# Sums of the down projection parked in DRAM between its pieces, and one more group of seven products, in a hybrid DiT step on one Trainium2 core

## The chip, the cores and the metric

One NeuronCore of a Trainium2 chip runs the whole program. The metric is the device time of one execution in microseconds (us); of the kernel before three executions were timed, and one further execution was profiled.

## What is computed

One inference step of a diffusion backbone with one layer, for two groups of 128 tokens (context and latent) of width 2048, all in fp32: modulation from a conditioning vector, one input projection, two attention mixers, their merge, and then the part that the change touches, a squared-ReLU MLP of width 8192:

```python
h2 = rms_norm(x, norm2_w) * (1 + sc2) + sh2
x = x + g2 * (jnp.square(jax.nn.relu(h2 @ w_up)) @ w_down)
```

The products keep nearly fp32 precision: every operand is split into a high part that fp32r holds exactly and a low part (the rest), and one product of two 128-row tiles is three matmuls: high by high, high by low, low by high.

## The kernel before, in words

All weights stream once from DRAM in tiles of 128 x 1024 fp32 (512 KB). One such tile is a **step**, and the kernel first writes a list of 456 steps (`wsteps`) and then records them in order in `run`. A step has a load (`raw`, in SyncE's queue, SP), a preparation (ScalarE copies `raw` to `wH`, L103; VectorE subtracts to `wL`, L269) and its matmuls. Two strings of digits set how far the recording runs ahead: at step i the loads up to step i + 4 + `RUN[i]` are issued and the preparations up to step i + `LOOK[i]` are recorded. All engines run their queues in order, and all tiles live in one pool of 50 buffers of 4 KB per partition (`G`), so a load waits in SP's queue until the buffer that it was given is free. For a few steps the low part is made by a GpSimd DMA that adds into it (`LO_DMA`), or the high part is loaded by a GpSimd DMA (`HI_DMA`, empty before).

The MLP is cut into eight pieces of 1024 hidden columns. After the up projection of piece 0, for p = 0 to 6, the up projection of piece p + 1 (`up_pair`, a **pair**, 16 steps) comes ahead of the down projection of piece p (`down_unit`, four units n = 0 to 3 of four steps each, one for each 512 output columns), and the down projection of piece 7 ends the program. So pair 1 is steps 216 to 231, down projection 0 steps 232 to 247, pair 2 steps 248 to 263, down projection 1 steps 264 to 279, pair 3 steps 280 to 295, and so on in 32s.

A pair has eight groups of two steps. A **plain** group does 8 products (24 matmuls) from two `wH`/`wL` tiles. A **fast** group forms sums of weight and activation blocks so that 7 products (21 matmuls, into Q1 to Q7) do the work of 8, in Winograd's manner; ScalarE makes `XH`, half of `YB`, `tH` and `uH`, and VectorE the other half of `YB`, `t`, `XL`, `tL`, `uL` and two half-width sums (L1315 to L1325). `FAST` names the places (0 to 7) of the fast groups in each pair: 34 fast groups in all.

The down projection's partial sums, 128 x 1024 for each n, are carried from piece to piece. ScalarE copies the two PSUM banks of a finished unit into `dsum[n]`, and three steps ahead of the next piece's unit n (`SEED_AT`; for n = 0 at the end of the pair) it copies them back into PSUM (`seed`), where the next matmuls add to them. So four of the 50 buffers hold `dsum` through the whole MLP.

Beside this, VectorE works off dot products of the conditioning vector with columns of the modulation weights (L1476, tiles `aT`), one job of two instructions per entry of `DOTS`/`DOTS2`, which give the step.

In the input projection `SEED1` says for each unit of a later chunk whether its earlier sum is copied into PSUM ahead of it by ScalarE, or added after it by VectorE.

Of the kernel before, what the change touches and what calls it, by code (L numbers as in the profile page):

```python
# [10 lines left out]
F32 = mybir.dt.float32  # L11
# [7 lines left out]
P = 128  # L19
# [12 lines left out]
LOAD = 4  # L32
FB_DVE = 2
FB1 = 10
H_AT = 3
FILL = {1: [("gB", 2), ("gB", 3)], 3: [("gB", 0), ("gB", 1)]}
DOTS1 = [9, 11, 14, 19, 22, 24, 25, 27, 28, 30, 32, 33, 34, 35, 37, 40, 41, 42, 44, 46, 48, 49, 51, 53]
CHUNKS = [2, 2, 2, 4, 6]
NFAST = 8
FAST = {1: (0, 2, 5, 7), 2: (0, 4, 5, 6, 7), 3: (0, 2, 4, 5, 7), 4: (0, 2, 4, 5, 7), 5: (0, 1, 3, 4, 7), 6: (0, 3, 4, 5, 7), 7: (0, 1, 3, 6, 7)}  # L40
SEED_AT = 3
QK_ACT = [('qB', 1)]
H2_DVE = [(0, 1), (0, 3), (1, 1), (1, 3)]
KEEP = True
ROWS_AT = [8, 11, 7]
SEED1_AT = 2
SEED1 = "111110100100111111011111111001011111"
BACK = 9
AWAY = [('gA', 1), ('gB', 2), ('gB', 3), ('gA', 0), ('gB', 0), ('gA', 2)]
GATE_BACK = 1  # L50
# [1 line left out]
LO_DMA = [50, 54, 56, 63, 77, 107, 129, 144, 145, 176, 184, 188, 189, 203, 228, 233, 250, 286, 297, 360, 388, 392, 403, 447]  # L52
LO_AHEAD = 2

LOOK = "610013015100121312024402233324102425654224523344556654121016645565652437574377445343414661516353205210022636320000411134313643044023400458230315565645456443574337324421522555644666784051000205311111322534111433455554321045445111013410444324654734331001335565775443654453304436533423355423455542233213213545587654334232213213202440122544412433432313432443523324313211333435533333213331314344422557756822145342656433332302254541454475574464555546763333345544"
RUN = "345110004667224234111350007998421004464200022565595544243214333434399864346555377654224635443144230021224242114401324405201346530331035587986564665545676867644543555342013141147676676965699967265287998988511453877787785653022200123446553345324545104653232464345673321110102122521121211202355533232133432223443232410110000000011234344212022112531112752123301000112323643331133410100122454235566436675432012021222210010001154457832224556577677636445664422134"
CONST_AT = [83, 79]
XL_DMA = [8]
HI_DMA = []
ADA_AT = [None, 4, 13, 22, 25]  # L60
XS_AT = {1: 3, 2: 25, 3: 34}
POST = {('kvA', 0): [81, 83, 89], ('qA', 0): [84, 86, 92], ('qA', 1): [84, 86, 90], ('kB', 0): [88, 92, 96], ('qB', 0): [94, 98, 104], ('kB', 1): [98, 101, 103], ('qB', 1): [102, 106, 107]}
# [2 lines left out]
T_AT = [4, 4]  # L65
PREP_IN = [5, 7]
DOTS = [44, 58, 58, 61, 62, 63, 65, 66, 66, 66, 69, 70, 71, 71, 72, 74, 76, 81, 84, 85, 89, 91, 94, 96, 96, 96, 100, 100, 101, 102, 102, 105, 107, 107, 107, 110, 110, 111, 113, 114, 115, 117, 117, 117, 120, 120, 120, 121, 121, 123, 123, 124, 127, 128, 128, 132, 132, 133, 133, 134, 135, 136, 141, 143, 144, 144, 149, 151, 151, 152, 157, 157, 157, 162, 163, 170, 172, 174, 174, 174, 176, 176, 178, 182, 183, 187, 190, 190]
DOTS2 = [224, 231, 231, 233, 235, 237, 238, 242, 245, 263, 265, 269, 275, 296, 299, 304, 309, 329, 331, 331, 333, 333, 353, 360, 362, 364, 366, 368, 382, 391, 394, 396]
STAT_AT = [-2, -1, 8, 17]
T_PAIR = [[7, 10], [6, 9], [8, 9], [8, 9], [10, 14], [10, 10], [11, 14]]  # L70
P_PAIR = [[5, 5], [2, 2], [2, 4], [6, 2], [4, 2], [4, 4], [6, 0]]
M_TE = (3,)
M_AT = [4, 6, 9]
FLIP = 1
P_UP = [2, 3]
T_UP = [6, 12]
COL = {"qA": 0, "kvA": 1024, "qB": 1536, "kB": 2560, "vB": 3584, "gA": 4608, "gB": 6656}


# [1 line left out]
def tile_hybrid_step(ctx: ExitStack, tc: tile.TileContext, a):  # L81
# [8 lines left out]
    dp = ctx.enter_context(tc.tile_pool(name="dram", bufs=1, space=bass.MemoryType.DRAM))  # L90
    act, dve, pe, pool, sync = nc.scalar, nc.vector, nc.tensor, nc.gpsimd, nc.sync

    def G(name, dt=F32):
        return gp.tile([P, 1024], dt, name=name, tag="g")
# [4 lines left out]
    def bank(name, pool_=None):  # L99
        return (pool_ or paux).tile([P, 512], F32, name=name, tag="b")  # L100

    def copy(out, in_):
        act.activation(out, in_, AF.Copy)  # L103
# [112 lines left out]
    wsteps = []  # L216
    cal = {}

    def at(i, fn):
        cal.setdefault(i, []).append(fn)  # L220
# [9 lines left out]
    def add_step(src, mm, key, half=0):  # L230
# [409 lines left out]
    def unit(w, c0, ktiles, stat, evac, key, seeded=None):  # L640

        box = {}
        n = len(ktiles)
        for j, k0 in enumerate(ktiles):
            def mm(st, j=j):
                if j == 0 and st["half"] == 0:
                    box["acc"] = seeded() if seeded else [bank("acc", pacc) for _ in range(2)]
                mm3(box["acc"], stat(j), st, j == 0 and st["half"] == 0 and not seeded, j == n - 1 and st["half"] == 1,
                    bool(seeded))
                if j == n - 1 and st["half"] == 1:  # L650
                    evac(box["acc"])
            add_w(w, k0, c0, mm, key)
# [323 lines left out]
    def up_flip(n):  # L976
        flip(("a", n))
# [45 lines left out]
    for u in AWAY:  # L1023
        i = end_of(("y" + u[0][1].lower(), u[1]))
# [156 lines left out]
    def up_unit(n):  # L1181
# [66 lines left out]
    def up_pair(p):  # L1248
        n0, n1 = PIECES[p]
        w, box, key = a["w_up"], {"begun": set()}, ("up", n0)  # L1250
        fast = FAST[p]

# [28 lines left out]
        for pos, is_fast in enumerate(kinds):  # L1281
# [16 lines left out]
            def prep_x(b=b, pos=pos):  # L1298
                b["XH"] = b["x"].pop("hi", None)
                if b["XH"] is None:  # L1300
                    b["XH"] = G("XH", F32R)
                    copy(b["XH"], b["x"]["raw"])
                if 8 * p + pos in XL_DMA:
                    b["XL"] = G("XL", F32R)
                    minus_plus(b["XL"], b["XH"], b["x"]["src"])

            def prep_y(b=b, pos=pos):
# [11 lines left out]
                dve.tensor_tensor(Y[:, 0:512], t[:, 0:512], X[:, 512:1024], op=OP.add)  # L1319
                if 8 * p + pos not in XL_DMA:  # L1320
                    dve.tensor_tensor(b["XL"], X, b["XH"].bitcast(F32), op=OP.subtract)
# [50 lines left out]
            for i, (nm, pf, mf) in enumerate((("x", prep_x, mm_x), ("y", prep_y, mm_y))):  # L1372
# [4 lines left out]
                else:  # L1377
                    assert wsteps[-1]["i"] not in HI_DMA
                wsteps[-1]["prep"] = pf

    dsum = {}
    last = len(PIECES) - 1

    def out_s(acc, n, ss, c=slice(0, 512)):
# [2 lines left out]
            out = a["y_prompt"] if s == 0 else a["y_sample"]  # L1387
            sync.dma_start(out[0][:, n * 512 + c.start:n * 512 + c.stop], x1[n][:, s, c])

    seeds = {}  # L1390

    def seed(p, n):

        seeds[p, n] = [bank("acc", pacc) for _ in range(2)]
        for s in range(2):
            copy(seeds[p, n][s], dsum[n][:, s, :])
        if p == last:
            dsum.pop(n)

    def down_unit(p, n):  # L1400
        def evac(acc):
            if p == 0:
                dsum[n] = G(f"dsum{n}").rearrange("p (s n) -> p s n", s=2)
            if p == last:
                out_s(acc, n, range(2))
                return
            for s in range(2):
                copy(dsum[n][:, s, :], acc[s])

        def stat(j):  # L1410
            return lambda kk, tb: (aH[PIECES[p][j]][:, kk, tb, :], aL[PIECES[p][j]][:, kk, tb, :])

        def seeded():
            if (p, n) not in seeds:
                seed(p, n)
            return seeds.pop((p, n))
        if p and (n or p == last):
            at(len(wsteps) - SEED_AT, lambda: seed(p, n))
        if p == last and n == 3:
            last_unit(a["w_down"], 512 * n, [4 * j for j in PIECES[p]], stat, lambda acc, s, *c: out_s(acc, n, [s], *c), ("down", p, n), seeded)  # L1420
            return
        unit(a["w_down"], 512 * n, [4 * j for j in PIECES[p]], stat, evac, ("down", p, n), seeded if p else None)

    for n in PIECES[0]:
        up_unit(n)
    for n in range(4):
        at(end_of(("up", 0)) + 1 + n, lambda n=n: x1_away(n))
    for g in range((max(len(f) for f in FAST.values()) + 1) // 2):
        at(end_of(("up", 0)) + STAT_AT[g], lambda g=g: fast_stat(g))
    for p in range(len(PIECES)):  # L1430
        if p < last and p + 1 not in FAST:
            for n in PIECES[p + 1]:
                up_unit(n)
        elif p < last:
# [106 lines left out]
    i = ROWS_AT[0] + max(i for i, (job, h, n) in placed if job[0] == "g1")  # L1541
# [115 lines left out]
```

## Time and profile before

| | |
|---|---|
| time, median of 3 executions | 1315.3 us (1315.15 to 1315.69) |
| profiled execution: its time / span of its instructions | 1315.33 / 1313.6 us |
| TensorE (PE) busy | 1300.4 us, 99% |
| VectorE (DVE) busy | 1147.2 us, 87% |
| ScalarE (ACT) busy | 918.3 us, 70% |
| DMA packets of the weights' queue | 378.18 MB, 78.8% of 16 engines' span |

The page's slices of 1/40 show where an engine is full, the windows the same for chosen stretches, the lines what one instruction costs, and the waits what held an engine or a queue up. A matmul's shown duration overlaps the next one's, so its price is the distance from start to start.

### The profile page before, as it was taken

Reading aid. Unit: us, or ns where it says so; the run is one execution under the profiler, and the core shown is the slowest. Engines: PE = TensorE matmul, PEld = TensorE weight load, DVE = VectorE, ACT = ScalarE, POOL = GpSimd, SP = SyncE. Lnnn points to the kernel's source line nnn. Section 1 sums busy time; section 2 is a strip of 40 time slices with the busy share of each in tenths; the row PEclk is TensorE's granted clock in tenths of the full one; section 3 lists DMA queues with packets and bytes.
Section 4 is the critical chain, followed back from the end, with each engine's and each line's share of the span. In section 5 each row is a group of like instructions: output and inputs, shape, how many; then the busy total and the mean of one; then the engine's idle time right before and its main releaser. Section 6 shows DMA issues by size and latency. Waiting matters only on the chain.

```text
span 1313.6 us, 17446 instructions
## 1 busy us (share of the span) xinstructions
PE 1300.4 (99%) x5978; PEld 1051.6 (80%) x5978; DVE 1147.2 (87%) x1531; ACT 918.3 (70%) x1299; POOL 60.9 (5%) x67
## 2 busy tenths in 40 slices
PE   8999999999999999999999999999999999999998
PEld 4677888888777788888888888888888888888886
DVE  4578999999999999999879998897989998979653
ACT  5656766698865566645687857869678687796881
POOL 0000000341100000000000000000000000000000
PEclk9999999999999999999999999999999999999999
DMA  9999998898899999999398775888586697867692
GB/s 372 408 408 409 378 363 320 314 339 287 294 338 364 411 377 353 363 353 379 104 331 305 256 252 173 280 286 285 198 302 226 209 319 249 295 160 303 195 352 79
DMA packets 148313, 393.80 MB, mean 300 GB/s; under 512 B 51680, under 2 KB 52672, under 8 KB 148224
## 3 DMA queue, kind: packets, MB, share of 16 engines
q1 hardware_dynamic: 144064, 378.18, 78.8%
q0 software_dynamic: 4016, 14.42, 5.7%
q8 instruction: 47, 0.77, 0.2%
q14 instruction: 42, 0.34, 0.1%
q10 hardware_dynamic: 144, 0.08, 0.0%
HBM read 373.97 MB, written 8.70 MB: 291 GB/s over the span
## 4 chain that ended last, share of the span: by engine, by line
PE 64%; DVE 4%; issue 1%; DVEq 0%
PE acc L321 13%; PE acc L322 13%; PE acc L320 13%; PE Q L1260 6%; PE Q L1258 6%; PE Q L1259 6%; DVE junk L1476 1%; DVE aT L1476 1%; DVE wL L269 1%; PE Z L1260 1%; PE Z L1258 1%; PE Z L1259 1%; PE acc L1096 1%; PE acc L1095 1%; PE acc L1078 1%
## 5 line engine op out<-in xcount | busy, mean ns | idle before, releaser
L269 DVE TENSOR_TENSOR wL<-raw,wH 128x1024 fp32r<-128x1024 f32 x361 | 425.6, 1223 | 63.9 <-ACT wH L103 63.0
L103 ACT ACTIVATE wH<-raw 128x1024 fp32r<-128x1024 f32 (+1 forms) x391 | 388.2, 1044 | 59.7 <-DMA raw<-in_w_br_a 8.4
L1476 DVE SCALAR_TENSOR_TENSOR aT<-aT,cB 128x1024 f32<-128x1024 f32 x144 | 173.7, 1222 | 1.1
L1476 DVE SCALAR_TENSOR_TENSOR junk<-aT,cB 128x1024 bf16<-128x1024 f32 x144 | 173.7, 1223 | 0.0
L451 PE MATMUL acc<-wH,hH 128*128 128x512 f32 x276 | 108.2, 392 | 0.0
L453 PE MATMUL acc<-wH,hL 128*128 128x512 f32 x276 | 107.5, 389 | 0.0
L452 PE MATMUL acc<-wL,hH 128*128 128x512 f32 x276 | 107.4, 389 | 0.0
L103 ACT ACTIVATE uH<-raw 128x1024 fp32r<-128x1024 f32 x34 | 36.1, 1063 | 65.1 <-DVE raw L1322 59.5
L451 PEld LDWEIGHTS acc<-wH,hH 128*128 128x128 f32 x276 | 51.8, 188 | 13.9 <-issue 2.5
L453 PEld LDWEIGHTS acc<-wH,hL 128*128 128x128 f32 x276 | 51.8, 188 | 10.8
L452 PEld LDWEIGHTS acc<-wL,hH 128*128 128x128 f32 x276 | 51.8, 188 | 10.6
L103 ACT ACTIVATE tH<-t 128x1024 fp32r<-128x1024 f32 x34 | 36.0, 1058 | 29.0 <-DVE t L1315 26.8
L320 PE MATMUL acc<-wH,hH 128*128 128x512 f32 x128 | 52.7, 411 | 0.0
L321 PE MATMUL acc<-wL,hH 128*128 128x512 f32 x128 | 50.2, 392 | 1.3 <-DVE wL L269 1.3
L486 PE MATMUL acc<-wH,hH 128*128 128x512 f32 x128 | 50.5, 395 | 0.0
L487 PE MATMUL acc<-wL,hH 128*128 128x512 f32 x128 | 50.0, 391 | 0.3 <-DVE wL L269 0.2
L322 PE MATMUL acc<-wH,hL 128*128 128x512 f32 x128 | 50.0, 391 | 0.0
L488 PE MATMUL acc<-wH,hL 128*128 128x512 f32 x128 | 49.9, 390 | 0.0
L1325 DVE TENSOR_TENSOR uL<-raw,uH 128x1024 fp32r<-128x1024 f32 x34 | 41.7, 1225 | 1.1
L1315 DVE TENSOR_TENSOR t<-raw 128x1024 f32<-128x1024 f32 x34 | 41.4, 1218 | 1.3 <-PE Q L1259 1.3
L1324 DVE TENSOR_TENSOR tL<-t,tH 128x1024 fp32r<-128x1024 f32 x34 | 41.4, 1217 | 0.0
L103 ACT ACTIVATE acc<-dsum 128x512 f32<-128x512 f32 x56 | 31.6, 590 | 13.8 <-DVE up L1360 7.1
(648 smaller groups left out, 3337.7 us busy)
## 6 DMA issues: line engine op xcount, KB each, us to landing
raw<-in_w_in SPq DMA_DIRECT2D x133, 512.0 KB, 8.2
raw<-in_w_down SPq DMA_DIRECT2D x128, 512.0 KB, 6.0
aT<-in_w_adaT SPq DMA_DIRECT2D x80, 512.0 KB, 8.4
raw<-in_w_upF SPq DMA_DIRECT2D x68, 512.0 KB, 5.3
aT<-in_w_gT SPq DMA_DIRECT2D x64, 512.0 KB, 8.0
raw<-in_w_up SPq DMA_DIRECT2D x60, 512.0 KB, 6.2
araw<-in_w_pair SPq DMA_DIRECT2D x48, 512.0 KB, 9.2
raw<-in_w_out SPq DMA_DIRECT2D x32, 512.0 KB, 9.6
```

The costliest lines, as they stand in the source:

```text
L103: act.activation(out, in_, AF.Copy)
L269: dve.tensor_tensor(st["lo"], st["raw"], st["hi"].bitcast(F32), op=OP.subtract)
L320: pe.matmul(acc[tb], sh, wh[:, k, :], start=f, stop=False, skip_group_check=seeded)
L321: pe.matmul(acc[tb], sh, wl[:, k, :], start=False, stop=False, skip_group_check=seeded)
L322: pe.matmul(acc[tb], sl, wh[:, k, :], start=False, stop=l, skip_group_check=seeded)
L451: pe.matmul(acc[tb], sh, wh[:, k, :], start=opened[u] and k == 0, stop=False, skip_group_check=skip)
L452: pe.matmul(acc[tb], sh, wl[:, k, :], start=False, stop=False, skip_group_check=skip)
L453: pe.matmul(acc[tb], sl, wh[:, k, :], start=False, stop=last and k == 1, skip_group_check=skip)
L1258: pe.matmul(acc, stat[0], hi, start=f, stop=False)
L1259: pe.matmul(acc, stat[0], lo, start=False, stop=False)
L1260: pe.matmul(acc, stat[1], hi, start=False, stop=l)
L1476: dve.scalar_tensor_tensor(out, box["raw"], 1.0, cB[s, tag], op0=OP.mult, op1=OP.mult, accum_out=dst[:, s, fb:fb + 1])
```

## The change

The sums of a unit are now copied into a new buffer `dpart`, stored to DRAM six steps after the unit (`SUM_AWAY`), and loaded again ten steps ahead of the unit that goes on with them (`SUM_BACK`), all in SP's queue. That is so for the down projections 0 to 5; what down projection 6 leaves stays in SBUF as before. Pair 2 has one more fast group, at its place 2 (steps 252 and 253), which makes 35; in pair 7 the fast group at place 6 moves to place 4. The high part of step 234 comes by a GpSimd DMA. `LOOK` changes in 51 places, 35 of them in steps 239 to 289, and `RUN` in 60: in steps 238 to 294 it changes at 52 and rises at 44 of them (for the 16 steps of down projection 1 it reads 3211101021225211 before and 1685756597166055 after), and outside that stretch only eight digits change, by one. Four dot jobs move later, from steps 245, 263, 265 and 275 to 265, 265, 267 and 279. Of the input projection's second chunk one unit (`qB`, 0) is added by VectorE instead of copied in ahead. `H_AT` enters a maximum that another term decides.

```diff
-H_AT = 3
+H_AT = 4
...
-FAST = {1: (0, 2, 5, 7), 2: (0, 4, 5, 6, 7), 3: (0, 2, 4, 5, 7), 4: (0, 2, 4, 5, 7), 5: (0, 1, 3, 4, 7), 6: (0, 3, 4, 5, 7), 7: (0, 1, 3, 6, 7)}
+FAST = {1: (0, 2, 5, 7), 2: (0, 2, 4, 5, 6, 7), 3: (0, 2, 4, 5, 7), 4: (0, 2, 4, 5, 7), 5: (0, 1, 3, 4, 7), 6: (0, 3, 4, 5, 7), 7: (0, 1, 3, 4, 7)}
...
-SEED1 = "111110100100111111011111111001011111"
+SEED1 = "111010100100111111011111111001011111"
...
+SUM_AWAY = 6
+SUM_BACK = 10
...
-HI_DMA = []
+HI_DMA = [234]
...
-T_PAIR = [[7, 10], [6, 9], [8, 9], [8, 9], [10, 14], [10, 10], [11, 14]]
+T_PAIR = [[7, 10], [6, 9], [8, 9], [8, 10], [10, 14], [10, 10], [11, 14]]
...
-T_UP = [6, 12]
+T_UP = [6, 14]
...
     def seed(p, n):
 
         seeds[p, n] = [bank("acc", pacc) for _ in range(2)]
         for s in range(2):
             copy(seeds[p, n][s], dsum[n][:, s, :])
-        if p == last:
-            dsum.pop(n)
+        dsum.pop(n)
+
+    def sum_away(p, n):
+        dmem[n] = dp.tile([P, 1024], F32, name=f"dm{p}_{n}")
+        sync.dma_start(dmem[n], parts.pop(n).rearrange("p s n -> p (s n)"))
+
+    def sum_back(n):
+        t = G(f"dsum{n}")
+        sync.dma_start(t, dmem.pop(n))
+        dsum[n] = t.rearrange("p (s n) -> p s n", s=2)
 
     def down_unit(p, n):
+        if 0 < p < last:
+            i = len(wsteps) - SUM_BACK
+            assert i > sum_end[n] + SUM_AWAY
+            at(i, lambda: sum_back(n))
         def evac(acc):
-            if p == 0:
-                dsum[n] = G(f"dsum{n}").rearrange("p (s n) -> p s n", s=2)
             if p == last:
                 out_s(acc, n, range(2))
                 return
+            t = G(f"dpart{n}").rearrange("p (s n) -> p s n", s=2)
             for s in range(2):
-                copy(dsum[n][:, s, :], acc[s])
+                copy(t[:, s, :], acc[s])
+            (dsum if p == last - 1 else parts)[n] = t
...
         unit(a["w_down"], 512 * n, [4 * j for j in PIECES[p]], stat, evac, ("down", p, n), seeded if p else None)
+        if p < last - 1:
+            sum_end[n] = len(wsteps) - 1
+            at(sum_end[n] + SUM_AWAY, lambda: sum_away(p, n))
```

The first place is SP's queue from the end of down projection 0's loads through those of pair 2 to the first ones of down projection 1 (`upF` is a fast group's weights, `up` a plain one's). Before:

```order
L243 DMA raw<-in_w_upF 128x1024 x2
L243 DMA raw<-in_w_up 128x1024 x6
L243 DMA raw<-in_w_upF 128x1024 x8
L243 DMA raw<-in_w_down 128x1024 x2
L1463 DMA aT<-in_w_gT 128x1024
```

With the change, from the first store on, which stands behind the first two `upF` and one `up` (`dm_n` is the place in DRAM of sum n):

```order
L1403 DMA dm_0_6976<-dpart_6829 128x1024
L245 DMA raw<-in_w_up 128x1024
L245 DMA raw<-in_w_upF 128x1024 x2
L245 DMA raw<-in_w_up 128x1024 x2
L245 DMA raw<-in_w_upF 128x1024
L1403 DMA dm_1_7086<-dpart_6930 128x1024
L245 DMA raw<-in_w_upF 128x1024 x4
L1403 DMA dm_2_7152<-dpart_7026 128x1024
L245 DMA raw<-in_w_upF 128x1024 x3
L245 DMA raw<-in_w_down 128x1024 x2
L1403 DMA dm_3_7272<-dpart_7112 128x1024
L1407 DMA dsum_7288<-dm_0_6976 128x1024
```

The four stores stand between pair 2's loads, and the first sum's return stands behind the second load of down projection 1. The same pattern comes for each of the six down projections, 48 DMAs in all.

The second place is VectorE's queue at the start of pair 2's preparations (`t` to `uL` is a fast group, `wL` half of a plain one, `aT` and `junk` half of a dot job). Before:

```order
L269 TENSOR_TENSOR wL<-raw,wH 128x1024
L1315 TENSOR_TENSOR t_7021<-raw 128x1024
L1318 TENSOR_TENSOR YB<-raw,YB 128x512
L1319 TENSOR_TENSOR raw<-t_7021,raw 128x512
L1321 TENSOR_TENSOR XL<-raw,XH 128x1024
L1322 TENSOR_TENSOR raw<-raw 128x512
L1324 TENSOR_TENSOR tL<-t_7021,tH 128x1024
L1325 TENSOR_TENSOR uL<-raw,uH 128x1024
L1476 SCALAR_TENSOR_TENSOR aT,gc_g_362<-aT,cB_6289 128x1024
L1476 SCALAR_TENSOR_TENSOR junk,gc_g_362<-aT,cB_6287 128x1024
L1476 SCALAR_TENSOR_TENSOR aT,gc_g_362<-aT,cB_6289 128x1024
L269 TENSOR_TENSOR wL<-raw,wH 128x1024 x5
```

With the change, from the end of the first fast group:

```order
L1327 TENSOR_TENSOR uL<-raw,uH 128x1024
L271 TENSOR_TENSOR wL<-raw,wH 128x1024
L1317 TENSOR_TENSOR t_7172<-raw 128x1024
L1320 TENSOR_TENSOR YB<-raw,YB 128x512
L1321 TENSOR_TENSOR raw<-t_7172,raw 128x512
L1323 TENSOR_TENSOR XL<-raw,XH 128x1024
L1324 TENSOR_TENSOR raw<-raw 128x512
L1326 TENSOR_TENSOR tL<-t_7172,tH 128x1024
L1327 TENSOR_TENSOR uL<-raw,uH 128x1024
L271 TENSOR_TENSOR wL<-raw,wH 128x1024 x2
```

The new fast group's seven instructions stand where two `wL` and the dot halves stood; the dot halves come later. (Step 250's low part is one of those that GpSimd makes, so a `wL` fewer than steps is seen in both.)

## Rows read from the trace of the kernel before

**Rows 1.** The page: span, the engines' busy time, granted clock in 40 slices, DMA rate.
```profile
span 1313.6 us, 17446 instructions
...
PE 1300.4 (99%) x5978; PEld 1051.6 (80%) x5978; DVE 1147.2 (87%) x1531; ACT 918.3 (70%) x1299; POOL 60.9 (5%) x67
...
PEclk9999999999999999999999999999999999999999
...
GB/s 372 408 408 409 378 363 320 314 339 287 294 338 364 411 377 353 363 353 379 104 331 305 256 252 173 280 286 285 198 302 226 209 319 249 295 160 303 195 352 79
```

**Rows 2.** Windows; stretch: its length, busy us of each engine, clock, DMA share, GB/s.
```profile
40.00:400.00 360.00, 356.60 (x1704) 284.19 (x1701) 327.39 (x501) 260.71 (x535) 40.83 (x34) 1.00 0.94 350
...
660.00:1220.00 560.00, 560.00 (x2472) 463.35 (x2471) 504.55 (x574) 428.68 (x477) 8.72 (x10) 1.00 0.78 260
```

**Rows 3.** Windows of down projection 0, pair 2, down projection 1 and pair 3.
```profile
719.00:763.00 44.00, 44.00 (x196) 36.44 (x195) 42.21 (x56) 35.97 (x37) 0.86 (x1) 1.00 0.80 263
763.00:804.00 41.00, 41.00 (x183) 33.95 (x182) 39.30 (x44) 24.24 (x29) 0.00 (x0) 1.00 0.64 236
804.00:848.00 44.00, 44.00 (x195) 36.21 (x194) 36.77 (x44) 39.96 (x46) 0.00 (x0) 1.00 0.69 232
848.00:889.00 41.00, 41.00 (x183) 33.95 (x182) 38.62 (x43) 26.72 (x30) 1.73 (x2) 1.00 0.86 290
```

**Rows 4.** Timeline of PE inside pair 3: start, us, engine, line, instruction.
```profile
852.85 0.39 PE L1258 MATMUL Q<-wH,h22H 128*128 128x512 f32 x1
...
853.30 0.39 PE L1260 MATMUL Q<-wH,h22L 128*128 128x512 f32 x1
```

**Rows 5.** Lines of DVE, 719 to 848 us: busy us, mean ns of one, idle before.
```profile
L269 DVE TENSOR_TENSOR wL<-raw,wH 128x1024 fp32r<-128x1024 f32 x34 | 39.8, 1219 | 4.6 <-ACT wH L103 4.6
L1476 DVE SCALAR_TENSOR_TENSOR aT<-aT,cB 128x1024 f32<-128x1024 f32 x12 | 14.6, 1222 | 0.2
...
L1325 DVE TENSOR_TENSOR uL<-raw,uH 128x1024 fp32r<-128x1024 f32 x6 | 7.4, 1225 | 0.3
...
L1318 DVE TENSOR_TENSOR YB<-raw,YB 128x512 fp32r<-128x512 f32 x6 | 4.1, 685 | 1.0 <-ACT YB L103 1.0
```

**Rows 6.** Lines of ACT, 719 to 848 us.
```profile
L103 ACT ACTIVATE wH<-raw 128x1024 fp32r<-128x1024 f32 x37 | 36.6, 1050 | 0.7 <-PE acc L321 0.7
...
L103 ACT ACTIVATE dsum<-acc 128x512 f32<-128x512 f32 x16 | 8.9, 592 | 3.6 <-PE acc L322 3.4
...
L103 ACT ACTIVATE tH<-t 128x1024 fp32r<-128x1024 f32 x6 | 6.4, 1059 | 8.3 <-DVE t L1315 8.3
```

**Rows 7.** Timeline, 796 to 813 us: DVE and PE at the end of pair 2.
```profile
810.18 2.36 DVE L269 TENSOR_TENSOR wL<-raw,wH 128x1024 fp32r<-128x1024 f32 x2 [2.02 <-ACT wH L103]
...
811.18 0.39 PE L320 MATMUL acc<-wH,a3H 128*128 128x512 f32 x1
811.46 0.50 PE L321 MATMUL acc<-wL,a3H 128*128 128x512 f32 x1
```

**Rows 8.** DMA issues: times, KB each, median us from issue to landing.
```profile
raw<-in_w_down SPq DMA_DIRECT2D x128, 512.0 KB, 6.0
...
x1d<-x SPq DMA_DIRECT2D x4, 512.0 KB, 5.8
x1b<-x1d SPq DMA_DIRECT2D x4, 512.0 KB, 9.0
```

**Rows 9.** Timeline: SP's issues around pair 2, and ACT's first seed of down projection 1.
```profile
743.26 15.56 SPq L243 DMA_DIRECT2D raw<-in_w_up  x6
...
781.45 0.80 SPq L243 DMA_DIRECT2D raw<-in_w_down  x2
...
784.37 10.79 SPq L243 DMA_DIRECT2D raw<-in_w_down  x2
...
800.48 0.60 ACT L103 ACTIVATE acc<-dsum 128x512 f32<-128x512 f32 x1
```

**Rows 10.** Waits of SP's queue, 700 to 900 us: who, total us, times, longest.
```profile
SPq L243 <- PE acc L322: 37.7, 10, 10.0
```

More of the change, by code (lines that the diff above doesn't have):

```diff
@@ L53 @@
 LO_AHEAD = 2
-LOOK = "610013015100121312024402233324102425654224523344556654121016645565652437574377445343414661516353205210022636320000411134313643044023400458230315565645456443574337324421522555644666784051000205311111322534111433455554321045445111013410444324654734331001335565775443654453304436533423355423455542233213213545587654334232213213202440122544412433432313432443523324313211333435533333213331314344422557756822145342656433332302254541454475574464555546763333345544"
-RUN = "345110004667224234111350007998421004464200022565595544243214333434399864346555377654224635443144230021224242114401324405201346530331035587986564665545676867644543555342013141147676676965699967265287998988511453877787785653022200123446553345324545104653232464345673321110102122521121211202355533232133432223443232410110000000011234344212022112531112752123301000112323643331133410100122454235566436675432012021222210010001154457832224556577677636445664422134"
+LOOK = "621013115100132423024402233324102425654224523344556654121016645565652437574377445343414661516353205210022636321100411134214643044023400458230315565645456443574337324421522555644666784051000205311111322534111433455554321045445111013410444325655447552012566586753333654465104465534314677412345542233213213545587654334232213213201330122544412533432313432443523324313211333435533333213331314344422557756822145342656433332302254541454475574464555546763333345544"
+RUN = "345110005667224234111350007998421004464200022565595544243214333434399864346555377654224635443144230021224242114401324405201346530331035587986564665545676867644543555342013141147676676965699967265287998988511453877787785653022200123446553356638964043754784798623683168575659716605554544645555755432133432223443232410110000000011234344212022112531112752123301000112323643331133410210122454235566326664332012021222210010001154457832224556577677636445664422134"
 CONST_AT = [83, 79]
+SUM_AWAY = 6
+SUM_BACK = 10
 XL_DMA = [8]
-HI_DMA = []
+HI_DMA = [234]
 ADA_AT = [None, 4, 13, 22, 25]
@@ L67 @@
 DOTS = [44, 58, 58, 61, 62, 63, 65, 66, 66, 66, 69, 70, 71, 71, 72, 74, 76, 81, 84, 85, 89, 91, 94, 96, 96, 96, 100, 100, 101, 102, 102, 105, 107, 107, 107, 110, 110, 111, 113, 114, 115, 117, 117, 117, 120, 120, 120, 121, 121, 123, 123, 124, 127, 128, 128, 132, 132, 133, 133, 134, 135, 136, 141, 143, 144, 144, 149, 151, 151, 152, 157, 157, 157, 162, 163, 170, 172, 174, 174, 174, 176, 176, 178, 182, 183, 187, 190, 190]
-DOTS2 = [224, 231, 231, 233, 235, 237, 238, 242, 245, 263, 265, 269, 275, 296, 299, 304, 309, 329, 331, 331, 333, 333, 353, 360, 362, 364, 366, 368, 382, 391, 394, 396]
+DOTS2 = [224, 231, 231, 233, 235, 237, 238, 242, 265, 265, 267, 269, 279, 296, 299, 304, 309, 329, 331, 331, 333, 333, 353, 360, 362, 364, 366, 368, 382, 391, 394, 396]
 STAT_AT = [-2, -1, 8, 17]
-T_PAIR = [[7, 10], [6, 9], [8, 9], [8, 9], [10, 14], [10, 10], [11, 14]]
+T_PAIR = [[7, 10], [6, 9], [8, 9], [8, 10], [10, 14], [10, 10], [11, 14]]
 P_PAIR = [[5, 5], [2, 2], [2, 4], [6, 2], [4, 2], [4, 4], [6, 0]]
@@ L1379, in up_pair @@
                 wsteps[-1]["prep"] = pf
-    dsum = {}
+    dsum, dmem, parts = {}, {}, {}
     last = len(PIECES) - 1
@@ L1388, in out_s @@
             sync.dma_start(out[0][:, n * 512 + c.start:n * 512 + c.stop], x1[n][:, s, c])
-    seeds = {}
+    seeds, sum_end = {}, {}
     def seed(p, n):
```

## The prediction

> **What bounds the kernel now.** I read the page first, then the windows, then single instructions. The span is 1313.6 us and TensorE is busy 1300.4 us of it, at the full granted clock (2.4 GHz) in every slice [rows 1]. The windows say where the other 13 us are: 3.4 us between 40 and 400 us, and none at all between 660 and 1220 us, which is the MLP up to the last pair, the stretch that the change works on [rows 2]. A busy TensorE need not be a full one, because a matmul's shown 0.39 us overlaps the next one. So I counted starts: 2472 matmuls in 560 us is 0.2265 us from start to start, and inside a run of them two starts are 0.45 us apart over two matmuls [rows 2, 4]. The mean is the pitch of an unhindered run; there is no hidden gap. TensorE's instruction count alone sets the time of this stretch, and a change there can win only by issuing fewer matmuls. It can lose by making one wait.
>
> Here a rule speaks otherwise: the Trainium skill, Perfetto Trace Analysis, Identifying the Most-Contended Engine, calls matmul busy time a poor measure and wants the busy share of weight loads. That share is 463.35 of 560 us, 83% [rows 2]; by that measure a sixth of the stretch, some 96 us, could still be had from operands that come earlier. The pitch speaks against it here.
>
> What stands close behind TensorE is VectorE. In down projection 0 and pair 2 it is busy 42.21 of 44 and 39.30 of 41 us, in down projection 1 36.77 of 44, in pair 3 38.62 of 41 [rows 3]. At the end of pair 2 its lead is used up: the first of two low parts that it starts at 810.18 is done after 1.2 us, and the matmul that reads it starts at 811.46, 0.28 us after the one before instead of 0.23 [rows 7]. That is a loss of 0.05 us, but it shows that the schedule has nothing in hand at that place.
>
> **The change part by part.**
>
> *The 35th fast group.* A plain group issues 24 matmuls, a fast one 21. Three fewer at 0.2265 us [rows 2] is **-0.68 us**, all of it on the path. Moving pair 7's fast group from place 6 to 4 changes no count: 0.
>
> *VectorE's share of it.* A fast group costs it four full-width instructions at about 1.22 us and three half-width ones at about 0.685, 6.9 us; the two `wL` that it replaces cost 2 x 1.219 = 2.4 us [rows 5]. So +4.5 us in down projection 0 or pair 2, which have 3.5 us idle between them [rows 3]. But two dot jobs leave this stretch: four instructions at 1.22 us, 4.9 us together [rows 5]. Net -0.4 us there, and +4.9 us in down projection 1, where 7.2 us are idle [rows 3]; a further job moves on from 275 to 279. So VectorE fits, with 2 us over in down projection 1. Its cover is look-ahead: it must work ahead during down projection 1, which needs buffers, and the parked sums give some back (each is away from six steps after its unit to ten steps ahead of the next, 12 of 32 steps). Price taken: 0. If the lead is not there, the unpaid part is at most the 4.5 us.
>
> *ScalarE.* The fast group costs three full-width copies and a half one, about 3.7 us, for two `wH` at 1.05: +1.6 us; step 234's high part by DMA gives 1.05 back [rows 6]. It is busy 24.24 of 41 us in pair 2 [rows 3]: 0. The copies out of PSUM are as many as before (0.592 us each), only to another tile.
>
> *The stores.* 24 sums of 512 KB. In SP's queue a store waits for its copy out, and the weight loads behind it wait too. In the trace down projection 0 runs from 719 to 763 us [rows 3], so its first unit ends a quarter in, near 730 us, and the load that now stands ahead of its store was issued at 743.26 or later [rows 9]. So the store finds its data ready by some 13 us. The tightest is sum 3, ready just behind the last unit, about 764; the two `w_down` loads ahead of its store went out at 781.45, and deeper look-ahead can bring that forward by some steps, not by 17 us, since SP is held by buffers that matmuls free (37.7 us in 10 waits, the largest entry of its queue) [rows 9, 10]. Price: 0.
>
> *The returns.* The nearest rows are the plain park and return of the residual in the same queue: 5.8 us for a store, 9.0 us for a load of what was stored [rows 8]. The return of sum 0 stands just ahead of a load that went out at 784.37, and ScalarE's seed of that sum starts at 800.48 [rows 9]: 16 us for a transfer of 9. For n = 1 to 3 the return stands ten steps ahead and the seed three; seven steps of 12 matmuls are 19 us. Price: 0, from below 0 excluded (nothing is taken away), from above the amount by which a return is later than 16 us.
>
> *DMA bandwidth.* 48 transfers and the extra load of step 234 are 49 x 0.524 = 25.7 MB, over the 515 us or so from the first store to the last return 50 GB/s on top of 260 at a share of 0.78 [rows 2]. At the page's best rate, 411 GB/s [rows 1], one transfer takes 1.3 us, 64 us in all, so the share goes to 0.9. Loads then land later by one or two transfers, 1.3 to 2.6 us, and are not short over the stretch as a whole. Price: between 0 and what the first rival says; I take 0, because SP's waits are for buffers and not for DMA [rows 10], and VectorE's in this stretch for ScalarE [rows 5].
>
> The Trainium skill, DMA: Bandwidth & Descriptors, Specifications, gives a core about 358 GB/s of HBM. By that ceiling pair 3's 290 GB/s plus 50 would leave almost nothing. The trace disagrees with it as a limit for this lone core: slices run at 408 to 411 [rows 1].
>
> *Outside the MLP.* The unit (`qB`, 0) loses four ScalarE copies (0.59 each [rows 6]) and gains two VectorE additions (0.69 each, by the half-width row [rows 5]); VectorE is busy 327 of 360 us there, TensorE lacks 3.4 us [rows 2]. Anything between +0.5 and -0.5 us; I take 0.
>
> **Sum.** The profiled execution took 1315.33 us, the same as the median of 1315.3. 1315.3 - 0.68 = **1314.6 us**. A measurement of this kernel can tell about 0.2%, 2.6 us, from no change, so this forecast is "no change that can be told".
>
> **The rivals.**
>
> 1. *Weights land late (slower).* The six parks and returns are four stores and four loads each, but look-ahead was deepened only in steps 238 to 294. For down projections 2 to 5, 16 sums go out and come back in front of loads that run no further ahead than before. Each pair of transfers delays what is behind it by 2.6 us. It decides where VectorE is no more than that ahead of TensorE, as at 811 us [rows 7]. If one sum in four costs its place 1.3 us, that is 4 x 1.3 = 5.2 us: 1319.8 us. For it: the share of 0.86 in pair 3 already [rows 3]. Against it: no VectorE wait for DMA heads the list [rows 5]. Chance 0.07.
> 2. *VectorE becomes the bound in pair 2 (slower).* The deeper look-ahead doesn't find its buffers, the dot jobs come back on it in down projection 1 with 2 us over, and most of the 4.5 us appears on TensorE: 1314.6 + 3 to 4.5, about 1318.5 us. For it: the lost lead in rows 7. Against it: the two moved jobs outweigh the group. Chance 0.06, half of it beyond 0.2%.
> 3. *The freed buffers take waits away (faster).* If the sixth in which TensorE loads no weights were waiting, operands that come earlier would win up to 96 us of it. The pitch leaves only the 3.4 us between 40 and 400 us [rows 2], which the MLP's buffers do not touch: at the very most 1314.6 - 3.4 = 1311.2 us. The rule named above would stand behind more. Chance 0.03.
> 4. *It doesn't do what it says.* If the returns were later than their seeds, TensorE would stop at every unit: 20 or more stalls of some us, over 1340 us. The 16 and 19 us speak against it: 0.01.
>
> **How the numbers follow.** The forecast has 0.83. "Same" takes it and half of rival 2: 0.86. Slower takes rivals 1 and 4 and the other half: 0.11. Faster is rival 3: 0.03. The range runs from 1313.6 (the 0.68 us, 0.5 us in the early stage, and the 0.5 us between executions) to 1317.2, which holds one or two late places of 1.3 us; beyond it lie the full rivals 1 and 2, about one case in ten, and below it less.
>
> **What would show it.** The changed profile should have 24 stores of `dpart` and 24 loads of `dsum`, three matmuls fewer, TensorE without idle time between 660 and 1220 us, pair 2 as long as 6 x 21 + 2 x 24 matmuls (39.4 us) and a DMA share of about 0.9. VectorE should have less idle time in down projection 1 than 7.2 us. I am wrong if TensorE shows waits for `wL` or `uL`, and by their place: near steps 248 to 279 it is rival 2, behind a park or return in down projections 2 to 5 rival 1, at a seed rival 4.

## The result: slower by 0.3%, and the profile after

The change takes **1318.9 us** (median of 9, 1318.23 to 1319.68), the kernel before 1315.3 us (median of 9): ratio 1.0027, 95% interval 1.0018 to 1.0036. That is 3.6 us slower, outside the range of the forecast. The profiled execution took 1319.36 us with a span of 1317.3 us, 3.7 us more than the span of [rows 1].

The page of the change: span and busy time of the engines.

```profile
span 1317.3 us, 17567 instructions
...
PE 1300.6 (99%) x5974; PEld 1050.5 (80%) x5975; DVE 1152.1 (87%) x1538; ACT 918.5 (70%) x1296; POOL 62.1 (5%) x68
```

Windows of the change from pair 2 on, over the stretches of [rows 3] (pair 2 ends earlier, at 803), one down projection further, and the MLP with its last pair; columns as in [rows 2].

```profile
763.00:803.00 40.00, 38.89 (x171) 31.65 (x170) 37.78 (x41) 23.71 (x28) 0.00 (x0) 1.00 0.89 319
803.00:848.00 45.00, 44.54 (x196) 36.43 (x195) 39.39 (x49) 38.73 (x44) 0.00 (x0) 1.00 0.83 274
848.00:889.00 41.00, 40.84 (x180) 33.49 (x180) 37.00 (x42) 26.67 (x31) 1.72 (x2) 1.00 0.86 290
889.00:933.00 44.00, 43.39 (x192) 35.61 (x191) 36.33 (x42) 39.32 (x44) 0.00 (x0) 1.00 0.88 300
...
660.00:1300.00 640.00, 637.50 (x2805) 525.42 (x2804) 551.07 (x623) 484.72 (x541) 10.13 (x12) 1.00 0.87 296
```

TensorE, which before had no idle time between 660 and 1220 us [rows 2], now has some in every stretch from pair 2 on. The mean DMA share is 0.87, about what was forecast. PE's timeline gives the places. The first three rows are the end of pair 2; then come one place in down projection 1, the end of pair 3 and one place in down projection 2; in brackets the idle time before a matmul and who ended it.

```profile
797.92 0.39 PE L1262 MATMUL Q<-XH,h22L 128*128 128x512 f32 x1
798.65 0.49 PE L1260 MATMUL Q<-uH,sH 128*128 128x512 f32 x1 [0.35 <-ACT uH L105]
799.91 0.50 PE L1261 MATMUL Q<-uL,sH 128*128 128x512 f32 x1 [0.77 <-DVE uL L1327]
...
813.01 0.50 PE L323 MATMUL acc<-wL,a3H 128*128 128x512 f32 x1 [0.46 <-DVE wL L271]
...
884.87 0.50 PE L1261 MATMUL Q<-uL,sH 128*128 128x512 f32 x1 [0.16 <-DVE uL L1327]
...
900.73 0.50 PE L323 MATMUL acc<-wL,a4H 128*128 128x512 f32 x1 [0.61 <-DVE wL L271]
```

From start to start the step from 797.92 to 798.65 is 0.73 us, and 0.23 is the pitch, so 0.50 is lost, more than the bracket says. Counted in this way (the excess over 0.227 at every late matmul) the change loses 1.65 us at the end of pair 2 and 0.82 at 804 to 813: 2.5 us, **place A**. It loses 0.43 at the end of pair 3, 0.88 at 899.7, 0.43 at 1057.5 (end of pair 5) and 0.23 at 1073.9: 2.0 us, **place B**. The kernel before loses 0.17 us, at 811. So 4.5 - 0.2 - 0.68 (three matmuls fewer) = +3.6 us, against 3.6 measured (3.7 in the profiled span). The stage up to 660 us is the same within 0.3 us. What must be found is why operands are late at these two places.

**Place A.** VectorE's timeline in pair 2 of the change: start, us, engine, line, instruction.

```profile
783.58 1.23 DVE L1327 TENSOR_TENSOR uL<-raw,uH 128x1024 fp32r<-128x1024 f32 x1
786.79 1.22 DVE L1317 TENSOR_TENSOR t<-raw 128x1024 f32<-128x1024 f32 x1 [1.98 <-PE Q L1262]
...
798.63 1.23 DVE L1327 TENSOR_TENSOR uL<-raw,uH 128x1024 fp32r<-128x1024 f32 x1
```

VectorE works almost without a gap from 738 us to the last `uL`, but for one long wait, 1.98 us ahead of a `t`. That instruction reads only `raw`, and the releaser is a matmul into Q, which doesn't make `raw`: the wait is for the *buffer* that `t` is written to. In the buffers that the built program gives out, the `t` of the fifth of pair 2's six fast groups takes over the buffer of the third's `tH`, which that group's last matmuls free. The digits of `RUN` in pair 2 go from 4653232464345673 to 3754784798623683: ten of them rise, by up to five, so loads are issued up to 13 steps ahead and hold buffers. Two explanations: the deeper look-ahead took the buffers (theory A1), or VectorE simply has too much work with the 35th group (theory A2).

**Place B.** ScalarE's timeline at the end of pair 3, and once in pair 5.

```profile
876.65 1.06 ACT L105 ACTIVATE wH<-raw 128x1024 fp32r<-128x1024 f32 x1 [2.02 <-DMA raw<-in_w_down]
...
878.72 0.61 ACT L105 ACTIVATE YB<-raw 128x512 fp32r<-128x512 f32 x1
...
1054.43 1.06 ACT L105 ACTIVATE wH<-raw 128x1024 fp32r<-128x1024 f32 x1 [2.75 <-DMA raw<-in_w_down]
```

VectorE at the same place, and SP's issues ahead of it.

```profile
879.36 0.69 DVE L1320 TENSOR_TENSOR YB<-raw,YB 128x512 fp32r<-128x512 f32 x1 [2.91 <-ACT YB L105]
```

```profile
864.06 0.42 SPq L1403 DMA_DIRECT2D dm<-dpart  x1
864.58 0.40 SPq L1407 DMA_DIRECT2D dsum<-dm  x1
865.93 2.19 SPq L245 DMA_DIRECT2D raw<-in_w_down  x3
```

ScalarE's queue is in order. A `wH` of down projection 2, which TensorE doesn't need before 889, waits 2.02 us for its load; behind it stands the `YB` of pair 3's last fast group, needed much sooner; VectorE then waits 2.91 us for that `YB`, and TensorE gets `uL`, and afterwards `wL`, late. (The step is 297, one of those whose low part GpSimd makes; the kernel prepares these two steps early.) Its load is the second of the three, issued at 866.35 and landed 10.2 us later. Ahead of it, a store and a return were issued, and from these on the transfers land 1.3 us apart, at 872.8 (store), 874.0 (return), 875.3 and 876.6 (loads); ScalarE was ready at 874.6. Theory B1: these transfers make the load late. Theory B2: it would be late anyway, by the new tables.

The median landing of a `w_down` load went from 6.0 us [rows 8] to 7.7.

```profile
raw<-in_w_down SPq DMA_DIRECT2D x128, 512.0 KB, 7.7
...
dm<-dpart SPq DMA_DIRECT2D x24, 512.0 KB, 7.2
dsum<-dm SPq DMA_DIRECT2D x24, 512.0 KB, 8.4
```

### The profile page after: what moved, and what is told of

Read it like the earlier page. It is cut to its first block, busy times and chain, and to the rows that moved or that the text cites. A ratio compares the mean times of both kernels' runs of the same rounds, so it can differ in the third digit from the quotient of the medians.

```text
span 1317.3 us, 17567 instructions
## 1 busy us (share of the span) xinstructions
PE 1300.6 (99%) x5974; PEld 1050.5 (80%) x5975; DVE 1152.1 (87%) x1538; ACT 918.5 (70%) x1296; POOL 62.1 (5%) x68
## 4 chain that ended last, share of the span: by engine, by line
PE 62%; DVE 7%; DMA 3%; ACT 3%; issue 2%; SPq 0%; DVEq 0%; ACTq 0%
PE acc L323 13%; PE acc L324 13%; PE acc L322 13%; PE Q L1261 5%; PE Q L1260 5%; PE Q L1262 5%; DVE wL L271 2%; DMA raw<-in_w_down 2%; DVE junk L1493 1%; DVE aT L1493 1%; DMA aT<-in_w_gT 1%; ACT wH L105 1%; PE Z L1262 1%; PE Z L1261 1%; PE Z L1260 1%
## 5 line engine op out<-in xcount | busy, mean ns | idle before, releaser
L1317 DVE TENSOR_TENSOR t<-raw 128x1024 f32<-128x1024 f32 x35 | 42.7, 1220 | 2.2 <-PE Q L1262 2.0
L1326 DVE TENSOR_TENSOR tL<-t,tH 128x1024 fp32r<-128x1024 f32 x35 | 42.7, 1220 | 0.0
L1323 DVE TENSOR_TENSOR XL<-raw,XH 128x1024 fp32r<-128x1024 f32 x34 | 41.5, 1220 | 0.0
```

## The experiments

All edits are against the change. Times are medians; each ratio is to the kernel before on the same chip, with its 95% interval. The expectations have letters of their own: A there is A2 and B1 together, B the transfers alone, C and A' the group's work alone (A2), D is A1, E is B1. The parking was made selective by a tuple of down projections whose sums go away:

```diff
+PARK = (0,)
...
-        if 0 < p < last:
+        if p - 1 in PARK:
...
-            (dsum if p == last - 1 else parts)[n] = t
+            (parts if p in PARK else dsum)[n] = t
...
-        if p < last - 1:
+        if p in PARK:
             sum_end[n] = len(wsteps) - 1
```

**1. No sum leaves (`PARK = ()`), the rest as changed.**

> The change with all its tables and 35 groups, but no sum goes to DRAM: each unit's sum stays in its new SBUF buffer until its seed, so 48 transfers are gone. Theory A (two causes: VectorE has no lead left at the end of pair 2, about 2.4 us there; and weight loads that land late behind parked sums, about 1.9 us at the ends of pairs 3 and 5): the waits for w_down loads at the ends of pairs 3 and 5 go, the stall of pair 2 stays or grows because sums hold buffers longer; 1317.0 us or somewhat more. Theory B (the transfers alone cost all of it, pair 2's stall too): 1314.6 us. Theory C (the 35th group and VectorE alone): 1318.9 us as before, no change.

1320.39 us (4 runs, 1319.26 to 1321.44), ratio 1.0038 (1.0023 to 1.0053). No stall is left after 810 us, which speaks for B1. But pair 2 is worse: 1.0 us at 764, 2.9 us between 798.6 and 802.4, and then matmuls at half the clock (last section). Without parking the buffers are still scarcer: up to 803 us VectorE waits 2.7, 1.9 and 0.4 us for a buffer, always ahead of a `t`. Two of the four runs are near 1319.4 and two near 1321.3, so the median stands for neither.

**2. 34 groups, the rest as changed** (the entry of pair 2 in `FAST`).

```diff
-2: (0, 2, 4, 5, 6, 7)
+2: (0, 4, 5, 6, 7)
```

> The change with all its tables and the parked sums, but pair 2 has its old five fast groups (34 in all): 3 matmuls more, about 4.5 us of VectorE less in pair 2. Theory A: pair 2's stall of about 2.4 us goes, the later ones of 1.9 us stay: 1318.9 - 2.4 + 0.7 = 1317.2 us. Theory B: 1318.9 + 0.7 = 1319.6 us. Theory C: 1315.3 us.

1319.87 us (6 runs), 1.0032 (1.002 to 1.0044), and not the 1317.2 expected. The same 1.65 us are lost at 798.6 to 800.7, although VectorE has 4.5 us less to do, and 0.8 after it; place B is there too, 1.75 us. VectorE's timeline:

```profile
787.47 1.23 DVE L1317 TENSOR_TENSOR t<-raw 128x1024 f32<-128x1024 f32 x1 [4.98 <-PE Q L1262]
```

The work that was taken away came back as waiting for the buffer, 4.98 us for 1.98. Theory A2 falls for this kernel.

**3. Parking alone: `H_AT`, `FAST`, `SEED1`, `LOOK`, `RUN`, `HI_DMA`, `DOTS2`, `T_PAIR`, `T_UP` as before.**

> The kernel before with its own tables and 34 groups, and only the parking added (24 stores, 24 returns). Theory A: no stall in pair 2 beyond the 0.05 us of before, weight loads late at some ends of pairs: about 1315.3 + 1.9 = 1317.2 us. Theory B: 1315.3 + 4.3 = 1319.6 us. Theory C: 1315.3 us.

1316.51 us (10 runs, 1315.62 to 1317.05), 1.0009 (0.9999 to 1.0018). The interval includes 1; the point estimate is 1 us slower. Its profiled execution (1315.65 us, among its fastest) shows a single stall, 0.66 us at 1221.7. At place B it has none, although all sums leave. ScalarE's `wH` of step 297 doesn't wait, and its load (again the second one) landed in 5.2 us, at 871.9:

```profile
872.24 1.05 ACT L105 ACTIVATE wH<-raw 128x1024 fp32r<-128x1024 f32 x1
```

```profile
854.71 0.38 SPq L1403 DMA_DIRECT2D dm<-dpart  x1
856.53 0.33 SPq L1407 DMA_DIRECT2D dsum<-dm  x1
...
866.73 0.33 SPq L245 DMA_DIRECT2D raw<-in_w_down  x1
```

Its window of pair 3:

```profile
848.00:889.00 41.00, 41.00 (x183) 33.95 (x182) 37.70 (x42) 26.77 (x31) 1.73 (x2) 1.00 0.98 335
```

TensorE is never idle in it, nor in down projection 2, though more is moved than in the change (335 against 290 GB/s). Here the store and the return go out 12 and 10 us ahead of that load, and five other loads stand between. In the change SP is held for a buffer until 862.07 and then issues two loads, the store, the return and three loads between 863.2 and 867.3. So parking alone did no harm at this place in this execution; it did with the new tables, under which the transfers go out right in front of the load. Which digits matter isn't separated by any run, and the slower executions of this kernel have no profile.

**4. The group alone: the tables as before, `FAST` as changed, `PARK = ()`.**

> The kernel before with its own look-ahead and dot tables and only the 35th fast group in pair 2 added; sums stay in SBUF. Theory A: VectorE has 4.5 us more to do in pair 2 without the dot jobs moved away, so TensorE waits there by 2.4 to 4.5 us: 1315.3 - 0.7 + 2.4 to 4.5 = 1317.0 to 1319.1 us, all of it at the end of pair 2 and the start of down projection 1. Theory B: 1314.6 us. Theory C: like A.

1318.76 us (9 runs), 1.0025 (1.0015 to 1.0035). (Pair 7's fast group moves here too.) Here VectorE does bind: it is busy 39.69 of the 40 us from 763 on, doesn't wait for a buffer, and TensorE still loses 2.9 us between 797.2 and 801.3, by `XL`, `uH` and `uL`; half a clock follows (last section). Three dot instructions (761.34 to 764.9, 3.6 us) still stand ahead of the new group, and the last `uL` starts at 799.64, 3.5 us later than in run 8. So A2 fits the group without its preparations, and not the change.

**5. Pair 2's `RUN` as before, all else as changed** (16 digits out of the string).

```diff
 # RUN, digits of steps 248 to 263
-3754784798623683
+4653232464345673
```

> The change, with the 16 digits of RUN for pair 2's steps (248 to 263) as they were before, so weights are loaded two to five steps less far ahead there. Theory D (buffers: the weights that are loaded up to 13 steps ahead hold the buffers that the last two fast groups of pair 2 need, so VectorE starts them only when TensorE has used up the third; that costs the stall of 1.65 us at 798 us and most of the 0.73 us at 812): VectorE's 2.0 us wait for a matmul in pair 2 goes and 1.5 to 2.4 us with it: 1316.5 to 1317.4 us. Theory A' (it is VectorE's work for the 35th group): the stall stays, 1318.9 us.

1316.71 us (10 runs, 1314.96 to 1318.19), 1.0011 (1.0001 to 1.002). The stall at the end of pair 2 is gone and at 810 us 0.4 are left:

```profile
763.00:803.00 40.00, 40.00 (x179) 33.12 (x178) 39.60 (x44) 23.66 (x28) 0.00 (x0) 1.00 0.73 266
```

16 digits are worth 2.2 us by the medians and 2.1 us by the trace (place A, 2.5 to 0.4): theory A1. Place B stays and is larger in this profile, 1.6 us at 881.6 and 0.9 at 898.4; the profiled execution (1317.82 us) is one of the slowest of the ten.

**6. The same with 34 groups.**

> The same with the old five fast groups in pair 2 (34 in all). Theory D: no stall in pair 2 at all, so the time is that of shallow_pair2 plus 0.7 us for three more matmuls, less what is left of pair 2's stall there: 1317 us. Theory A': pair 2's stall goes only here, by 2.4 us against shallow_pair2.

1316.32 us (10 runs), 1.0009 (0.9999 to 1.0019). No stall in pair 2, and still 0.86 us at 897.5: what is left isn't the group's doing. With all sums parked, 35 groups (run 5) and 34 can't be told apart.

**7. Only down projection 0's sums leave (`PARK = (0,)`), `RUN` as changed.**

> The change with only the sums of down projection 0 parked (4 stores and 4 returns instead of 24 and 24); the others stay in SBUF from their unit to their seed. Theory E (late weight loads behind parks and returns make the stalls at the ends of pairs 3 and 5): ScalarE's waits for w_down loads of 2.0 and 2.75 us there go, and with them 1.9 us, pair 2 keeps its 2.4: 1317.0 us. If the later stalls come from pair 2's delay or from the tables alone, they stay: 1318.9 us.

1316.76 us (10 runs, 1316.51 to 1317.05), 1.0009 (1.0 to 1.0019). Place A is there to the hundredth (1.64 us at 797.9 to 800), place B is gone:

```profile
848.00:889.00 41.00, 41.00 (x182) 33.98 (x182) 38.71 (x45) 27.59 (x32) 1.72 (x2) 1.00 0.77 245
889.00:933.00 44.00, 44.00 (x196) 36.47 (x195) 36.09 (x41) 39.73 (x46) 0.00 (x0) 1.00 0.75 243
```

**8. Both: `PARK = (0,)` and pair 2's `RUN` as before.**

> Both: RUN of pair 2 as before and only the first down projection's sums parked, 35 groups. Theories D and E together: neither stall is left, 1314.6 to 1315.5 us. If either fails, 1317 us or more.

**1314.80 us** (10 runs, 1314.35 to 1315.57), 0.9995 (0.9986 to 1.0005). VectorE in pair 2, at the place of the 1.98 us:

```profile
783.12 1.22 DVE L1328 TENSOR_TENSOR uL<-raw,uH 128x1024 fp32r<-128x1024 f32 x1
784.26 1.22 DVE L1318 TENSOR_TENSOR t<-raw 128x1024 f32<-128x1024 f32 x1
...
796.10 1.23 DVE L1328 TENSOR_TENSOR uL<-raw,uH 128x1024 fp32r<-128x1024 f32 x1
```

The `t` follows at once (in this program it takes over the buffer of a plain group's `wL`, whose last matmul started at 782.23, 2 us earlier), and the last `uL` starts 2.5 us earlier. The windows of pair 2 and pair 3 are full again:

```profile
763.00:803.00 40.00, 40.00 (x178) 33.16 (x177) 39.59 (x44) 23.53 (x28) 0.00 (x0) 1.00 0.74 267
848.00:889.00 41.00, 41.00 (x183) 33.96 (x182) 37.64 (x42) 27.20 (x31) 1.72 (x2) 1.00 0.82 260
```

One stall of 0.4 us is left, at 810, where the kernel before lost 0.17 by the same count (0.05 of it in [rows 7]).

**9. No sum leaves, with pair 2's `RUN` as before.**

> 35 groups, RUN of pair 2 as before, no sum parked at all. Asks whether the parking is needed for the 35th group. If the four buffers of the first sums matter (theory D): VectorE waits for buffers early in pair 2, as it did 2.7 us in sums_stay, and TensorE waits 1 to 3 us there: 1316 to 1318 us. If the shallower loads alone make the room: 1314.8 us, as park_first_shallow.

1316.64 us (10 runs), 1.001 (1.0001 to 1.0019). VectorE waits 2.76 us for a buffer at 757, and TensorE loses 1.0 us at 764, 0.5 at 799 and 0.8 at 812. So the parking of the *first* sums does pay for the group: 1.8 us.

```profile
757.25 1.23 DVE L1318 TENSOR_TENSOR t<-raw 128x1024 f32<-128x1024 f32 x1 [2.76 <-PE acc L324]
```

**10. The sums of down projections 0 and 1 leave, with pair 2's `RUN` as before.**

> park_first_shallow with the sums of down projection 1 parked too (8 stores, 8 returns). Theory E, by place: these transfers lie in pair 3 and at the start of down projection 2, so ScalarE's wait for a w_down load at the end of pair 3 and the stall of 1.3 to 1.7 us come back there and nowhere else: 1314.8 + 1.5 = 1316.3 us. If the number of parks in all counts, not the place: 1315.2 us.

1316.0 us (10 runs, 1315.25 to 1316.62), 1.0005 (0.9996 to 1.0014). Stalls come back just behind the added sums, 0.98 us at 882.2 and 0.86 at 898.1, and nowhere else; the profiled execution (1316.62 us) is the slowest of the ten, so they are the upper end. ScalarE's wait:

```profile
875.07 1.06 ACT L106 ACTIVATE wH<-raw 128x1024 fp32r<-128x1024 f32 x1 [2.60 <-DMA raw<-in_w_down]
```

In run 8 the same instruction waits 0.30 us, and not for a DMA:

```profile
872.41 1.06 ACT L106 ACTIVATE wH<-raw 128x1024 fp32r<-128x1024 f32 x1 [0.30 <-PE Q L1263]
```

SP in run 10, then in run 8:

```profile
861.91 0.42 SPq L1404 DMA_DIRECT2D dm<-dpart  x1
862.43 0.40 SPq L1408 DMA_DIRECT2D dsum<-dm  x1
863.78 2.21 SPq L246 DMA_DIRECT2D raw<-in_w_down  x3
```

```profile
864.23 2.62 SPq L246 DMA_DIRECT2D raw<-in_w_down  x3
```

The loads are not issued later (the first at 863.78 against 864.23, the second at 864.20 against 866.04); they land later. From 860 to 877 us the loads of `raw` need this long (the view of one tile), in run 10 and then in run 8:

```profile
DMA to landing us min/median/max: 3.6/9.3/11.2
```

```profile
DMA to landing us min/median/max: 3.6/6.3/9.1
```

3.0 us more in the median, about the 2.6 us that the prediction gave two transfers in front. That is theory B1; by run 3 it needs the new tables as well.

**11. Run 8 again.**

> park_first_shallow once more with more rounds, to tell its 0.5 us from nothing: by the count of matmuls (-0.68 us) and its stall of 0.4 us at 810 us, 1315.3 - 0.68 + 0.2 = 1314.8 us.

1314.75 us (11 runs, 1314.59 to 1315.09), 0.9996 (0.9987 to 1.0005). It is the best version: about 4 us under the change. Against the kernel before it is 0.5 us lower in both batches, but neither interval excludes 1, so a gain over it is likely and not shown.

The two factors side by side, in us:

| `RUN` in pair 2 | no sum leaves | first sums only | all sums |
|---|---|---|---|
| as changed | 1320.39 | 1316.76 | 1318.9 |
| as before | 1316.64 | 1314.80 | 1316.71 |

Down a column the deeper look-ahead costs 3.8 (half a clock in it, last section), 2.0 and 2.2 us; from the first sums to all, 2.1 and 1.9 us. In the two right columns the costs add up: 1314.8 + 2.0 + 1.9 = 1318.7. The batches ran on different chips, where the kernel before took 1315.3 to 1315.5, and each interval is about 1.2 us to either side; that two differences of 2 us are two causes rests on the traces, where place A follows `RUN` and place B the parking.

## Why the prediction was wrong

- **The 35th fast group, -0.68 us: right, by the trace.** From the first matmul of pair 2 to the first of down projection 1 the kernel before takes 40.12 us (762.90 to 803.02), run 8 39.44 (762.29 to 801.73). The execution time alone can't show it: run 8 is 0.5 us under the kernel before, inside the interval.
- **"VectorE's share of it", price 0: wrong, about +2.2 us.** The failed step is "its cover is look-ahead: it must work ahead during down projection 1, which needs buffers, and the parked sums give some back". It counted the buffers that the sums give back and not those that deeper `RUN` takes, though both stand in the same diff. The busy time was estimated well: with the buffers there it fits (run 8, 39.59 us of 40, no stall), and with 34 groups the loss stayed (run 2). Rival 2 has the right place and, in its clause "the deeper look-ahead doesn't find its buffers", the right cause; its price was that of VectorE's work, 3 to 4.5 us, and not of the wait, 1.98. The chance of 0.06 was too low. [Rows 7] was read for the wrong place: 810 us is 7 us into down projection 1, and VectorE itself had waited there, 2.02 us for ScalarE's `wH`. At the end of pair 2 the trace of the kernel before shows a buffer wait of 1.32 us already, and the last `uL` done at 798.38, 0.8 us ahead of its first matmul:

```profile
785.31 1.23 DVE L1315 TENSOR_TENSOR t<-raw 128x1024 f32<-128x1024 f32 x1 [1.32 <-PE Q L1259]
...
797.16 1.22 DVE L1325 TENSOR_TENSOR uL<-raw,uH 128x1024 fp32r<-128x1024 f32 x1
...
799.16 0.39 PE L1259 MATMUL Q<-uL,sH 128*128 128x512 f32 x1
```

So little was in hand at that place, and a longer wait ahead of it had to show on TensorE.
- **"DMA bandwidth", price 0: wrong, about +2.0 us.** The share (0.9; 0.87 measured) and the delay (1.3 to 2.6 us; 1.7 in the median of the `w_down` loads, 3.0 locally in run 10) were about right; the reason given for 0 was "SP's waits are for buffers and not for DMA". That is a mean over a stretch. At each place one late load was enough, because in ScalarE's queue it stands ahead of work that is needed first (a `YB` at the end of pair 3, copies and seeds at the end of pair 5). This is rival 1 in its kind. Its place was half wrong: it exempted the steps up to 294, where look-ahead had been deepened, and the first and largest loss lies there, at the end of pair 3 and in down projection 2. Deeper look-ahead did not protect them; with the tables of before nothing was lost there (run 3). And in the profiled execution two places of six are hit, not four sums of sixteen: 2 us instead of 5.2. That rival 2's 1318.5 us lies near the measured time is luck: it is one cause overpriced, where two came.
- **Stores and returns, 0: right** as far as they themselves go. The first seed of down projection 1 runs at 802, 26 us after its return was issued at 775.97, and the one seed that makes TensorE stop (1057.38) waits for a VectorE `up` behind the late chain of pair 5, not for its return. A store took 7.2 us and a return 8.4 in the median, for the 5.8 and 9.0 taken. What they cost is the loads behind them, the point above.
- **ScalarE and the input projection, 0: right** within 0.3 us.
- **Rival 3 (buffers given back take waits away): as little as thought.** No kernel came under 1314.35 us. The rule of the Trainium skill (Perfetto Trace Analysis, Identifying the Most-Contended Engine), which judges headroom by MFU (the share of peak arithmetic) and by weight-load share, would by the latter see the same room in run 8 as before: PE's weight loads hold 33.16 of 40 us, 83%, in a window without a stall. The pitch was the better guide here.
- **The bandwidth rule was no help either way.** Pair 2 of the change moves 319 GB/s, pair 3 290, and loads are late in the second of them; before, pair 3 moved 290 as well [rows 3] and in run 3 335, both without a late load. By these runs what counts is which transfers go out just ahead of a load that is needed soon, not the mean rate. The page DMA: Bandwidth & Descriptors of the Trainium skill gives a core 358 GB/s (Specifications) and ties that, in a note under Bandwidth, to both cores of the HBM domain streaming; one core runs here, so its 408 to 411 GB/s [rows 1] don't contradict the page as the prediction has it.

The range was too narrow for the same reason in both places: two terms were taken at 0 without reading the reserve there (0.8 us at the end of pair 2; 2.4 at the end of pair 3, where the kernel before has its last `uL` done at 880.57 and reads it at 883.00), and each rival was priced as if the other could not come too.

What stays open: run 3's 1 us, which new digits put place B's transfers in the way, and why kernels in which all sums go out scatter over 1.4 to 3.2 us (runs 3 and 5) when those with the first sums only stay within 0.5 to 1.2 (runs 7, 8, 11).

## What to carry to other kernels

Prefetch depth and prepared operands draw on the same buffers: before deepening a load, find which instruction gets its buffer later by it, and whether the engine there has any lead. When transfers are put into a queue of loads, look at each load behind them for the in-order engine that takes it up, and at what waits behind *that* instruction; a mean share below 1 doesn't show it, and loads issued deeper can come to stand right behind the transfers. If a side measure is needed to feed one spot (here the sums of one down projection), apply it only there: the other 20 sums cost about 2 us with these tables and gave nothing.

## What the hardware showed that was not expected

In two kernels TensorE's stalls were followed by a lower clock. In run 4, at the end of pair 2, three waits (0.29, 1.01 and 0.76 us idle between 797.6 and 800.9) are followed by matmuls 0.43 us apart instead of 0.23. PE's timeline of that kernel, and its windows ahead of, in and after this stretch; the column after the engines is the granted clock:

```profile
800.91 0.50 PE L1262 MATMUL Q<-uL,sH 128*128 128x512 f32 x1 [0.76 <-DVE uL L1328]
...
801.48 0.62 PE L1261 MATMUL Q<-YB,h22H 128*128 128x512 f32 x1
801.90 0.63 PE L1262 MATMUL Q<-YB,h22H 128*128 128x512 f32 x1
```

```profile
790.00:798.00 8.00, 7.71 (x35) 6.07 (x33) 7.93 (x10) 3.77 (x5) 0.00 (x0) 1.00 0.39 141
801.50:804.80 3.30, 3.30 (x9) 2.61 (x8) 3.30 (x4) 2.03 (x4) 0.00 (x0) 0.50 1.02 407
806.00:812.00 6.00, 6.00 (x28) 4.94 (x28) 4.50 (x8) 4.57 (x5) 0.00 (x0) 1.00 0.15 60
```

The granted clock falls to 0.50 (1.2 GHz) and is back at 1.00 by 806. Nine matmuls take 3.3 us, where at 0.227 they take 2.0: 1.3 us in this window, on top of 2.9 lost by the stalls. Run 1 shows it too:

```profile
803.10:808.50 5.40, 5.40 (x14) 4.23 (x13) 4.06 (x5) 2.86 (x4) 0.00 (x0) 0.50 0.78 314
```

Fourteen matmuls in 5.4 us, 2.2 us lost. In the change the two waits at this place (0.35 and 0.77 us) left the clock at 1.00. So at a place without reserve a little more waiting can cost more than the wait itself; these are two profiled executions, and no run here varies the length of the waits alone.
